# Another constant, in the scheduler's model, for the part of a matmul step that does not depend on its columns

## The chip, the cores and the metric

The kernel runs on one core of one Trainium2 chip. The metric is the device time of one execution in microseconds (us); lower is better. Several runs of the same program are taken and their median is compared. Names of engines: PE is TensorE (PEld its weight loads), DVE VectorE, ACT ScalarE, POOL GpSimd, SP SyncE, which here only issues DMAs.

## The reference

Two layers of a hybrid trunk on 512 tokens of width 2048, in fp32. Each layer normalises x, projects it with one wide matrix, feeds two head groups (a gated linear attention and a chunked softmax attention), concatenates the gated heads, projects them out, normalises again and adds the result to x:

```python
def hybrid_layer(x, w_in, w_out, g_pre, g_post, ...):
    h = rmsnorm(x, g_pre)
    z = h @ w_in
    gq, gk, gv, gg, ga, aq, ak, av, ag = split_columns(z)
    log_a = jax.nn.log_sigmoid(ga @ w_alpha + b_alpha) / GLA_TAU
    o_gla = gla_chunk_causal(gq, gk, gv, log_a)
    o_gla = rmsnorm(o_gla, g_gla) * jax.nn.silu(gg)
    o_att = chunk_band_attention(aq, ak, av, rel_bias)
    o_att = rmsnorm(o_att, g_att) * jax.nn.silu(ag)
    y = jnp.concatenate([o_gla, o_att], axis=-1) @ w_out
    return x + rmsnorm(y, g_post)
```

## The kernel before

**Jobs.** The weights of both layers are cut into blocks, and every piece of 256 x 512 weights is one `Job` (class at line 135). A job has three parts. `load` (L144) issues DMAs on SP: one weight piece into a tile `raw` or `H` (L141) and, for some products, a stored left operand into a tile `sa` (L166). `high` (L168) forms sums of weight pieces on DVE where a product needs them (L176, L178, L180) and casts the result on ACT to a short format, the tile `wh` (L183). `low` (L185) subtracts on DVE what the cast has kept, which gives the tile `wl` (L187). Each product is then three matmuls: left-high by `wh`, left-high by `wl`, left-low by `wh`.

**Products.** `std_gemm` (L266; matmuls at L283) multiplies block by block. `fast_gemm` (L297; matmuls at L347 and L357) takes two column blocks together and forms seven products P1 to P7 of four pieces each in place of eight, with sums of operands formed beforehand. Those sums of left operands lie in DRAM (`S1` to `S4`, `A22`, and `oS...` for the output projection) and come back as the `sa` tiles.

**Other work beside the stream.** Attention heads, the linear attention, the norms and the transposes are Python generators that the gemms advance between jobs. At the end of a layer `finish` (L1118) runs `finish_token` (L1099): a sum of squares (L1101), a reciprocal root on POOL (L403), and four pieces of x + y*r on DVE (L1113). In layer 0 `prep_half` (L448) then normalises the new x (L456), transposes it on PE into one of four PSUM tiles `ax` (L466), evacuates each with two ACT instructions (L476) and splits it (L105, L106) into the left operands `a110`, `a120` and so on of layer 1.

**Two loads that share the SP queue.** `fetch_operands`, called after every piece of the last products of the input projection, loads what the attention heads have written to DRAM (`oa_d`, written at L804 from POOL's queue, one transfer for each two heads) for the output projection:

```python
def fetch_operands(k, c):
    passed.add((k, c))
    for i in range(4):
        if ("P1", 3) in passed and 2 * i in heads_done and (0, i) not in op_att:
            op_att[0, i] = slot(f"a11{i}", [2, 512], F32R)
            nc.sync.dma_start(flat(op_att[0, i]), oa_d[l][0, i])      # L1044
```

Its tiles are named a110 to a113; a112 belongs to heads 4 and 5, whose transfer to DRAM comes last.

**What sets the order.** The program is written once, in the order of the Python text. The framework then orders each engine's own instruction stream:

```python
with tile.TileContext(nc, schedule_with_timeline_sim=True) as tc:   # L1209
    hybrid_trunk(tc, *args)
```

It follows a modelled timeline of all engines and puts next on each engine what the model says comes up next. On the chip every engine works through its stream strictly in that order and waits on semaphores where an input is not there yet. Tile names carry running numbers (`wl_3096`, `sa_1142`), which stay the same when the order changes.

Of the kernel before, what the change touches and what calls it, by code (L numbers as in the profile page):

```python
# [6 lines left out]

F32 = mybir.dt.float32
F32R = mybir.dt.float32r
BF16 = mybir.dt.bfloat16  # L10
# [23 lines left out]
def hybrid_trunk(  # L34
# [29 lines left out]
    def nm(s):  # L64
        serial[0] += 1
        return f"{s}_{serial[0]}"

    def slot(tag, shape, dtype=F32):
        return slots.tile([P] + shape, dtype, tag=tag, name=nm(tag))

    def rtile(tag, shape=(2, W), dtype=F32, bufs=4):
        return ring.tile([P] + list(shape), dtype, tag=tag, name=nm(tag), bufs=bufs)

    def t2(shape=(512,), dtype=F32):
        return tmp.tile([P] + list(shape), dtype, tag="t2", name=nm("t2"))

    def ev():
        return tmp.tile([P, 512], F32, tag="ev", name=nm("ev"), bufs=6)

    def sgt(shape):  # L80
        return tmp.tile([P] + shape, F32, tag="sg", name=nm("sg"), bufs=2)

    def sm(cols, tag="sm", bufs=None):
        return small.tile([P, cols], F32, tag=tag, name=nm(tag), **({"bufs": bufs} if bufs else {}))

# [1127 lines left out]
```

## Time and profile before

| | |
|---|---|
| time, median of 3 runs | 1702.46 us (1696.93, 1702.46, 1706.23) |
| profiled execution, from its first to its last instruction | 1701.1 us; its own time is given only by this span |
| PE busy | 1648.9 us, 97% of the span |
| DVE, ACT, POOL busy | 1209.9, 873.2, 160.0 us |
| mean granted TensorE clock | 0.991 |

How to read the profile's lines: in a timeline a row is start, duration (us), engine, line of the kernel, operation, output<-inputs, count, and in brackets how long the engine sat idle before it and what ended that. A matmul's recorded 0.39 us overlaps its neighbours; the step from one to the next is what counts. The chain of waits is followed back from the last instruction; its rows are start, length and what filled it. The windows view gives, for a stretch of time, its length, each engine's busy time with the number of its instructions, then the granted PE clock, the DMA engines' busy share and GB/s.

### The profile page before, as it was taken

The page shows a single profiled execution, that of the slowest core. Times are in us where ns is not written, and L with a number is a line of the kernel's source. Part 1 is how long each engine was busy: PE and PEld are TensorE (multiplying, and loading weights), DVE is VectorE, ACT ScalarE, POOL GpSimd, SP SyncE. Part 2 cuts the span into 40 slices and gives each one's busy share as a digit, 9 for nine tenths or more (in the row PEclk, how much of TensorE's full clock was granted, in tenths as well). Part 3 has the DMA queues.
Part 4 walks back from the last instruction along what each step waited for, and adds up shares of the span by engine and source line. Part 5 has one row for each costly group of instructions (what it writes and reads, how often), then busy time and mean ns, then how long its engine had stood idle before and what let it go on. Part 6 is the DMA issues. An engine that isn't in the chain of part 4 may idle for free. (4 is left out here: it accounts for less than half of the span.)

```text
span 1701.1 us, 24915 instructions
## 1 busy us (share of the span) xinstructions
PE 1648.9 (97%) x9090; PEld 1403.5 (83%) x9090; DVE 1209.9 (71%) x1563; ACT 873.2 (51%) x1460; POOL 160.0 (9%) x256
## 2 busy tenths in 40 slices
PE   7999999999999999999999999999999999999995
PEld 5888878999987877787778878799999888777884
DVE  5846867686776876468887567668777667854886
ACT  8634544455665544345684345345556555433443
POOL 0210000001000101210122000000001001022101
PEclk8999999999999999999999999999999999999998
DMA  7986877868858797589779688868587678865993
GB/s 259 364 301 226 331 255 265 281 203 273 294 184 279 242 348 252 175 315 314 251 239 370 240 294 297 290 233 291 192 298 256 210 259 268 300 232 197 354 334 135
DMA packets 143002, 455.04 MB, mean 268 GB/s; under 512 B 15444, under 2 KB 32212, under 8 KB 142880
## 3 DMA queue, kind: packets, MB, share of 16 engines
q1 hardware_dynamic: 119984, 373.76, 64.2%
q0 software_dynamic: 22176, 78.41, 11.9%
q8 instruction: 72, 1.18, 0.3%
q10 hardware_dynamic: 720, 1.28, 0.2%
q14 instruction: 50, 0.41, 0.1%
HBM read 381.28 MB, written 72.11 MB: 267 GB/s over the span
## 5 line engine op out<-in xcount | busy, mean ns | idle before, releaser
L357 PE MATMUL mm<-wh,sa 128*128 128x512 f32 x1536 | 490.3, 394 | 9.1 <-ACT wh L183 4.0
L183 ACT CAST wh<-raw 128x1024 fp32r<-128x1024 f32 x248 | 261.8, 1057 | 276.8 <-PE mm L357 76.4
L187 DVE TENSOR_TENSOR wl<-raw,wh 128x1024 fp32r<-128x1024 f32 x248 | 301.8, 1221 | 96.5 <-PE mm L283 32.2
L357 PEld LDWEIGHTS mm<-wh,sa 128*128 128x128 f32 x1536 | 289.7, 189 | 74.5 <-ACT wh L183 5.8
L183 ACT CAST wh<-H 128x1024 fp32r<-128x1024 f32 x224 | 234.8, 1052 | 225.2 <-PE mm L357 123.9
L187 DVE TENSOR_TENSOR wl<-H,wh 128x1024 fp32r<-128x1024 f32 x224 | 272.3, 1221 | 93.8 <-PE mm L357 33.5
L357 PE MATMUL mm<-wl,sa 128*128 128x512 f32 x768 | 303.2, 395 | 9.5 <-DVE wl L187 9.4
L347 PE MATMUL mm<-sa,wh 128*128 128x256 f32 x1280 | 236.9, 285 | 0.0
L347 PEld LDWEIGHTS mm<-sa,wh 128*128 128x128 f32 x1280 | 200.2, 191 | 0.4
L357 PE MATMUL mm<-wh,a 128*128 128x512 f32 x576 | 184.0, 393 | 2.6 <-DVE t L319 2.6
L347 PE MATMUL mm<-sa,wl 128*128 128x256 f32 x640 | 181.3, 283 | 0.0
L357 PEld LDWEIGHTS mm<-wl,sa 128*128 128x128 f32 x768 | 145.4, 189 | 43.5 <-DVE wl L187 14.5
L283 PE MATMUL mm<-wh,a 128*128 128x512 f32 x512 | 169.4, 395 | 3.6 <-ACT a L105 1.8
L176 DVE TENSOR_TENSOR H<-H,raw 128x1024 f32<-128x1024 f32 x112 | 136.7, 1222 | 1.9
L357 PEld LDWEIGHTS mm<-wh,a 128*128 128x128 f32 x576 | 107.3, 188 | 25.1 <-DVE t L319 3.0
L347 PEld LDWEIGHTS mm<-sa,wl 128*128 128x128 f32 x640 | 122.5, 191 | 0.0
L180 DVE TENSOR_TENSOR raw<-H,raw 128x1024 f32<-128x1024 f32 x48 | 58.8, 1225 | 86.1 <-DMA raw<-in_w_dram 86.0
L403 POOL TENSOR_TENSOR sm<-sm,mhalf 128x2 f32<-128x2 f32 (+2 forms) x44 | 53.2, 1210 | 688.6 <-DVE sm L777 459.9
L283 PEld LDWEIGHTS mm<-wh,a 128*128 128x128 f32 x512 | 95.9, 188 | 26.0 <-ACT a L105 2.3
L357 PE MATMUL mm<-wl,a 128*128 128x512 f32 x288 | 113.5, 394 | 0.9 <-DVE wl L187 0.9
L283 PE MATMUL mm<-wl,a 128*128 128x512 f32 x256 | 100.5, 393 | 0.5 <-DVE wl L187 0.4
L347 PE MATMUL mm<-a,wh 128*128 128x256 f32 x512 | 94.8, 284 | 0.0
(193 smaller groups left out, 2350.9 us busy)
## 6 DMA issues: line engine op xcount, KB each, us to landing
raw<-in_w_dram SPq DMA_DIRECT2D x312, 512.0 KB, 5.2
sa<-S SPq DMA_DIRECT2D x192, 512.0 KB, 5.1
H<-in_w_dram SPq DMA_DIRECT2D x56, 512.0 KB, 4.8
sa<-A SPq DMA_DIRECT2D x48, 512.0 KB, 6.0
S<-g POOLq DMA_DIRECT2D x32, 512.0 KB, 7.8
oS<-g POOLq DMA_DIRECT2D x32, 512.0 KB, 7.1
sa<-oS SPq DMA_DIRECT2D x32, 512.0 KB, 5.5
sg<-t POOLq DMA_DIRECT2D x32, 256.0 KB, 5.5
```

The costliest lines, as they stand in the source:

```text
L176: nc.vector.tensor_tensor(out=h, in0=h, in1=r, op=ALU.add)
L180: nc.vector.tensor_tensor(out=r, in0=h, in1=r, op=ALU.subtract)
L183: last_cast[0] = nc.scalar.copy(self.wh, src).ins
L187: nc.vector.tensor_tensor(out=self.wl, in0=self.src, in1=self.wh.bitcast(F32), op=ALU.subtract)
L283: nc.tensor.matmul(pss[o], a[:, part, t], rhs[:, kk, :], start=(i == 0 and kk == 0 and m == 0), stop=(i == n - 1 and kk == 1 and m == 2),)
L347: nc.tensor.matmul(dst, lhs[:, kk, f], a[:, part, tok], start=(fresh and kk == 0 and m == 0 and ft % 2 == 0), stop=(c == 3 and kk == 1 and ...
L357: nc.tensor.matmul(out_ps[t], a[:, part, tok], rhs[:, kk, :], start=(fresh and kk == 0 and m == 0), stop=(c == 3 and kk == 1 and m == 2), ...
L403: nc.gpsimd.tensor_tensor(out=out_r, in0=v, in1=mhalf[:, : v.shape[-1]], op=ALU.pow)
```

## The change

Two lines behind the imports; no line of the kernel's own code changes:

```diff
 from concourse import mybir
 from concourse._compat import with_exitstack
 
+import concourse.hw_specs as _hs
+_hs.TRN2Spec.PE_FULL_CLOCK_PASS_GAP_NS = 13.3
 F32 = mybir.dt.float32
 F32R = mybir.dt.float32r
 BF16 = mybir.dt.bfloat16
```

The constant belongs to the model by which the framework orders the instructions: at PE's full clock a matmul's modelled step is its columns by the clock's period plus this constant. It was 2.5. The same instructions run on the same engines; only their order within an engine's stream moves. Lines of the changed kernel are two higher than before (L357 is L359). With that allowed for, 777 rows of PE's 7,200 odd stand differently, 439 lines of DVE's listing, 212 of ACT's, 64 of SP's and 6 of POOL's. Nearly all are swaps of neighbours. The three places that matter for what follows:

**SP, last products of layer 0's input projection.** Before, the load of a112 stands behind the left operands sa_1142 and sa_1145:

```order
L141 DMA raw_1155_6074<-in_w_dram 128x1024
L166 DMA sa_1142_5998<-S203_91 128x1024
L166 DMA sa_1145_6017<-S402_98 128x1024
L1044 DMA a112_1129_5934<-oa002_158 128x1024
L166 DMA sa_1148_6035<-S403_99 128x1024
```

Now it stands ahead of both:

```order
L143 DMA raw_1155_6074<-in_w_dram 128x1024
L1046 DMA a112_1129_5934<-oa002_158 128x1024
L168 DMA sa_1142_5998<-S203_91 128x1024
L168 DMA sa_1145_6017<-S402_98 128x1024
L168 DMA sa_1148_6035<-S403_99 128x1024
```

Layer 1 has the same move, of a112_2688 ahead of sa_2701 and sa_2704. So SP now reaches sa_1142 and sa_2701 only after the load of a112 has been issued.

**DVE, the last products of layer 1 with the final norms of tokens 0 to 255.** Before (wl_3091, wl_3096 and wl_3104 are the low parts of three consecutive pieces, L178 forms the sum of two pieces that is split next, L1113 the output):

```order
L187 TENSOR_TENSOR wl_3091_15717<-raw_3083_15676,wh_3087_15697 128x1024
L178 TENSOR_TENSOR raw_3088_15699<-raw_3088_15699,raw_3089_15701 128x1024
L1101 TENSOR_REDUCE sm_3102_15755<-ssy_2910_14855 128x1
L1088 TENSOR_TENSOR g1_3077_15652<-t2_3100_15750,t2_3004_15307 128x512
L1101 TENSOR_REDUCE sm_3106_15779<-ssy_2913_14867 128x1
L1113 SCALAR_TENSOR_TENSOR g6_2928_14915<-g8_2911_14857,sm_3103_15756,g6_2928_14915 128x1024
L1113 SCALAR_TENSOR_TENSOR g7_2929_14916<-g0_3074_15646,sm_3103_15756,g7_2929_14916 128x1024
L187 TENSOR_TENSOR wl_3096_15740<-raw_3088_15699,wh_3092_15720 128x1024
L1113 SCALAR_TENSOR_TENSOR g12_2930_14919<-g11_2914_14869,sm_3107_15780,g12_2930_14919 128x1024
L1113 SCALAR_TENSOR_TENSOR g13_2931_14920<-g1_3077_15652,sm_3107_15780,g13_2931_14920 128x1024
L178 TENSOR_TENSOR raw_3093_15722<-raw_3093_15722,raw_3094_15724 128x1024
L187 TENSOR_TENSOR wl_3104_15775<-raw_3093_15722,wh_3097_15743 128x1024
```

Now:

```order
L189 TENSOR_TENSOR wl_3096_15740<-raw_3088_15699,wh_3092_15720 128x1024
L180 TENSOR_TENSOR raw_3093_15722<-raw_3093_15722,raw_3094_15724 128x1024
L1103 TENSOR_REDUCE sm_3102_15755<-ssy_2910_14855 128x1
L1090 TENSOR_TENSOR g1_3077_15652<-t2_3100_15750,t2_3004_15307 128x512
L1103 TENSOR_REDUCE sm_3106_15779<-ssy_2913_14867 128x1
L1115 SCALAR_TENSOR_TENSOR g6_2928_14915<-g8_2911_14857,sm_3103_15756,g6_2928_14915 128x1024
L1115 SCALAR_TENSOR_TENSOR g7_2929_14916<-g0_3074_15646,sm_3103_15756,g7_2929_14916 128x1024
L189 TENSOR_TENSOR wl_3104_15775<-raw_3093_15722,wh_3097_15743 128x1024
L1115 SCALAR_TENSOR_TENSOR g12_2930_14919<-g11_2914_14869,sm_3107_15780,g12_2930_14919 128x1024
L1115 SCALAR_TENSOR_TENSOR g13_2931_14920<-g1_3077_15652,sm_3107_15780,g13_2931_14920 128x1024
L189 TENSOR_TENSOR wl_3108_15799<-H_2975_15128,wh_3105_15777 128x1024
```

The split wl_3096 and the sum raw_3093 have passed the norm's rows, and wl_3104 stands ahead of g12 and g13. Some rows earlier, the sum raw_3070 and one product with the gain (g1_3077) have moved ahead of the split wl_3081. The end of layer 0 has the same moves among its rows.

**PE, from layer 0 to layer 1.** Before, layer 1's first matmuls (wh_1586 by a110) come while eight of the 32 transposes of the first half of the tokens are left, and the other 24 stand in small groups among the matmuls ahead:

```order
L357 MATMUL mm_1450_7468<-wl_1585_8093,g17_1288_6692 128x512
L357 MATMUL mm_1450_7468<-wh_1567_8029,g17_1288_6692 128x512
L283 MATMUL mm_1614_8218<-wh_1586_8095,a110_1563_8002 128x512
L283 MATMUL mm_1614_8218<-wl_1595_8142,a110_1563_8002 128x512
L466 MATMUL ax_1590_8109<-cst_199,g6_1369_7069 128x128
L466 MATMUL ax_1590_8109<-cst_199,g12_1371_7073 128x128
```

Now 31 of the 32 stand in one block between the last matmul of layer 0 and the first of layer 1; its last rows are:

```order
L468 MATMUL ax_1590_8109<-cst_199,g12_1371_7073 128x128
L468 MATMUL ax_1593_8120<-cst_199,g7_1370_7070 128x128
L468 MATMUL ax_1593_8120<-cst_199,g13_1372_7074 128x128
L468 MATMUL ax_1593_8120<-cst_199,g7_1370_7070 128x128
L468 MATMUL ax_1593_8120<-cst_199,g13_1372_7074 128x128
L285 MATMUL mm_1614_8218<-wh_1586_8095,a110_1563_8002 128x512
L285 MATMUL mm_1614_8218<-wl_1595_8142,a110_1563_8002 128x512
```

So wh_1586 now stands behind the whole block, which fills eight PSUM tiles out of a pool of four.

## Prediction

> **What bounds the kernel now.** First the busy shares, then the chain of waits, which says what released whom.
>
> ```profile
> span 1701.1 us, 24915 instructions
> PE 1648.9 (97%) x9090; PEld 1403.5 (83%) x9090; DVE 1209.9 (71%) x1563; ACT 873.2 (51%) x1460; POOL 160.0 (9%) x256
> ...
> 1439.92 7.95 DMA sa<-S
> ...
> 1605.09 19.04 PE mm L357 x84
> ```
>
> PE has 97% of the span, and DVE, the next, 71%. The last row, from the chain, is an undisturbed stretch: 19.04 / 84 = 226.7 ns a matmul of 512 columns. The chain's row above it shows what else can set the end: PE out of work, here for an operand `sa` from DRAM. PE's matmuls are the same before and after, so their time stays; the change can act only through the waits of PE, and the sum below is one of waits. The span is 1701.1 us and the median of the runs 1702.46; the profiled execution is thus an ordinary one, 0.1% under the median, and I sum from 1701.1.
>
> First the constant itself. In the timeline, matmuls of 256 columns follow one another so:
>
> ```profile
> 353.98 0.40 PE L347 MATMUL mm<-sa,wh 128*128 128x256 f32 x2
> 354.22 0.28 PE L347 MATMUL mm<-sa,wl 128*128 128x256 f32 x1
> 354.34 0.40 PE L347 MATMUL mm<-sa,wh 128*128 128x256 f32 x2
> ```
>
> Three steps take 354.34 − 353.98 = 0.36 us, 120 ns each. So 256 more columns cost 226.7 − 120 = 106.7 ns, 512 cost 213.4, and 226.7 − 213.4 = 13.3 ns do not depend on the columns: the changed constant is what this trace says. The Trainium skill (TensorE: Matmul & The Clock Gate, "Wait — 56ns, not 53.3ns?") gives 2.5 ns for this part at full clock and 215.7 ns for 512 columns; the trace's 226.7 does not agree and decides. By the page the old model was right and the new one makes PE look 5% too slow, so that its inputs would be put too late; that is the last rival below. Either way no instruction becomes faster: the number enters the time only through the order.
>
> **A truer model is not yet a better order.** So I went through the moved rows by what each engine does in the trace.
>
> *Most swaps are in slack.* In the middle of the layers sums of weight pieces and small attention products pass a split `wl`. One of the tightest:
>
> ```profile
> 602.24 1.22 DVE L187 TENSOR_TENSOR wl<-raw,wh 128x1024 fp32r<-128x1024 f32 x1
> 603.37 0.42 DVE L106 TENSOR_TENSOR g<-t,g 128x256 fp32r<-128x256 f32 x1
> ...
> 603.72 0.40 PE L357 MATMUL mm<-wl,sa 128*128 128x512 f32 x1
> ```
>
> The split ends at 603.46, its first matmul starts at 603.72: slack 0.26. The product behind it (0.42, about 0.33 in step) now stands ahead, so PE loses under 0.1 us. Five more of these moves have slack close to their delay; elsewhere the delay of 0.6 to 1.2 us meets more slack than that. I put all of the middle at **+0.3**, between −1 (waits of this kind that happen to close) and +2 (six places at 0.33 each).
>
> *SP: a112 ahead of sa_1142 and sa_2701.* Here something real is put in line. The load of a112 reads what POOL's queue writes to `oa`:
>
> ```profile
> L804 POOL DMA_DIRECT2D oa<-g x1: 537/537/537, 602.6 to 602.6; - x1
> ...
> DMA to landing us min/median/max: 3.3/3.3/3.3
> ...
> 603.94 1.09 SPq L166 DMA_DIRECT2D sa<-S  x2
> 605.92 0.32 SPq L1044 DMA_DIRECT2D a<-oa  x1
> 606.34 0.53 SPq L166 DMA_DIRECT2D sa<-S  x1
> ...
> 609.88 0.47 PE L357 MATMUL mm<-wh,sa 128*128 128x512 f32 x1 [1.00 <-DMA sa<-S]
> ```
>
> POOL's transfer starts at 602.6 and lands 3.3 us later, at 605.9; a112 goes out at 605.92. It waits for that landing, and SP stands still meanwhile. Before, sa_1142 had left at 603.94, in front. Now it leaves where today the DMA behind a112 does, at 606.34, 2.4 us later. The last row is its first matmul: PE already sits idle 1.00 us for exactly this load. No slack is left, so if the load takes its 609.88 − 603.94 = 5.94 us again, PE loses 2.4 us. The same in layer 1:
>
> ```profile
> L804 POOL DMA_DIRECT2D oa<-g x1: 537/537/537, 1438.6 to 1438.6; - x1
> ...
> DMA to landing us min/median/max: 3.7/3.7/3.7
> ...
> 1439.92 1.21 SPq L166 DMA_DIRECT2D sa<-S  x2
> 1442.31 0.32 SPq L1044 DMA_DIRECT2D a<-oa  x1
> 1442.76 0.87 SPq L166 DMA_DIRECT2D sa<-S  x1
> ...
> 1448.01 0.51 PE L357 MATMUL mm<-wh,sa 128*128 128x512 f32 x1 [2.56 <-DMA sa<-S]
> ...
> sa<-S SPq DMA_DIRECT2D x192, 512.0 KB, 5.1
> ```
>
> sa_2701 would leave at 1442.76 instead of 1439.92, 2.84 later. It took 8.1 us to its matmul here, because four more transfers shared the DMA engines; the median `sa` takes 5.1 (last row). With 5.1 it would land at 1447.9 and cost nothing; with 8.1 at 1450.9, +2.8. The engines stay as full, so I take **+1.9** here, and **+2.4** for layer 0 (where 5.1 gives +1.6 and 8.1 gives +4.6). The other moves on SP, found by following each load to its first use, have 20 us and more to spare.
>
> *The granted clock.* Behind a long idle PE runs a while at about half clock:
>
> ```profile
> 609.00:613.50 4.50, 3.62 (x16) 2.99 (x17) 3.59 (x4) 2.08 (x3) 0.00 (x0) 1.00 1.03 418
> 1448.00:1451.40 3.40, 3.39 (x9) 2.67 (x10) 2.03 (x2) 0.00 (x0) 0.00 (x0) 0.54 1.02 348
> ```
>
> After 2.56 us of idle the clock was 0.54 for 3.4 us, which costs 3.4 x 0.46 = 1.6 us; after 1.00 us it stayed at 1.00. With 2.4 added, layer 0's idle is 3.4 us, so I add **+1.6** there, from 0 to 1.6. Layer 1 has paid already, and the ends of both layers are such places as well:
>
> ```profile
> 826.00:862.00 36.00, 32.25 (x148) 25.65 (x147) 32.08 (x45) 30.91 (x60) 7.66 (x14) 0.95 0.58 195
> ...
> 1646.00:1690.00 44.00, 37.86 (x157) 29.92 (x155) 33.32 (x39) 16.20 (x27) 3.60 (x7) 0.96 0.50 179
> ```
>
> There 36 x 0.05 and 44 x 0.04, both 1.8 us, go to the clock. The same page of the Trainium skill ("What's actually happening") has the clock fall after an idle window of about 3.4 us; here 2.56 was enough. By the page alone this +1.6 would be open, and the sum 1.6 lower.
>
> *The step from layer 0 to layer 1.*
>
> ```profile
> 830.69 0.80 PE L357 MATMUL mm<-wl,sa 128*128 128x512 f32 x1 [2.56 <-DVE wl L187]
> ...
> 841.50 1.55 ACT L476 ACTIVATE H<-ax,gcol 128x256 f32<-128x256 f32 x4
> ...
> 853.02 0.39 PE L283 MATMUL mm<-wh,a 128*128 128x512 f32 x1
> ...
> 853.48 1.03 PE L466 MATMUL ax<-cst,g 128*128 128x128 f32 x8
> ```
>
> The first idle, 2.56 us at 830.69, is a split that waits behind rows of the norm. With the splits ahead of the norm it shrinks, but the norm ends later and the transposes with it. Eight transposes take 0.8 us in step (853.48 to the next matmul at 854.27), and the other 24 hide among matmuls. Now 31 stand in a row with four PSUM tiles, so the second four need the first evacuated, two ACT instructions each at 1.55 / 4 = 0.39. One round of two tiles is 0.8 of evacuation and 0.8 of transposes; the block costs about 0.1 x 31 = 3.1 us plus some waiting, of which 0.8 was paid already: +2.5, first matmul of layer 1 at about 855.5 instead of 853.02. The low part of a110, a DVE row of 0.69, stands behind norm rows of the next tokens and costs about 1 more; what the earlier idle gives back is about 0.5. I take **+3**, from 0 (all of it regained from the 2.56) to +6.
>
> *The tail.*
>
> ```profile
> 1657.51 1.23 DVE L178 TENSOR_TENSOR raw<-raw,raw 128x1024 f32<-128x1024 f32 x1 [0.31 <-DMA raw<-in_w_dram]
> ...
> 1661.09 1.22 DVE L187 TENSOR_TENSOR wl<-raw,wh 128x1024 fp32r<-128x1024 f32 x1
> ...
> 1664.58 2.48 DVE L1113 SCALAR_TENSOR_TENSOR g<-g,sm,g 128x1024 f32<-128x1024 f32 x2 [0.40 <-POOL sm L403]
> 1666.97 1.22 DVE L187 TENSOR_TENSOR wl<-raw,wh 128x1024 fp32r<-128x1024 f32 x1
> ...
> 1672.89 1.23 DVE L187 TENSOR_TENSOR wl<-raw,wh 128x1024 fp32r<-128x1024 f32 x1 [1.17 <-ACT wh L183]
> ...
> 1668.25 0.49 PE L357 MATMUL mm<-wl,sa 128*128 128x512 f32 x1 [2.57 <-DVE wl L187]
> ...
> 1672.91 0.73 PE L357 MATMUL mm<-wh,sa 128*128 128x512 f32 x2 [2.12 <-ACT wh L183]
> ```
>
> wl_3096 starts at 1666.97 behind two norm rows (2.48) and PE waits 2.57 for it. Putting it ahead would save that. But the move of wl_3081 behind two other DVE rows (1.14 + 0.60 in step) and a later start of the first bring it 2.1 us later; its end frees the buffer of raw_3084, for which the first row above waits already. So the sum raw_3083 comes at about 1659.5, and splits and sums follow: wl_3091 at 1661.9 (+0.8), wl_3096 ends at 1667.2 instead of 1668.2 (−1.0), and wl_3104, now behind g6 and g7 but not g12 and g13, ends at 1674.8 instead of 1674.1. PE's next wait, at 1672.91, goes, and the one for wl_3104 comes in its place. I take **−0.5**, from −3 (the load of raw_3084 is on time all the same) to +1.5.
>
> **Sum:** +0.3 + 2.4 + 1.9 + 1.6 + 3 − 0.5 = +8.7 us; 1701.1 + 8.7 = **1710 us**, 0.5% up. Lower and upper ends of the six terms add to −2.4 and +18.5; I do not expect all on one side.
>
> **Rivals.**
> - *The splits that pass the norms win* (faster). If raw_3084 lands on time and the transposes find their tiles free, the idles of 2.56 at 830.69, 2.57 at 1668.25 and 2.12 at 1672.91 go, and with them the 1.8 of clock at each end: −10.9. With the two a112 terms at their low end (+1.6 and 0) this is −9.3, about **1692**. For it: these are the largest waits on DVE. Against: in both places the norm has to be done before what is next, and its rows are only moved.
> - *The queue on SP is not felt* (no change). If the `oa` transfer lands earlier, or the loads take 5.1 us, what stays is 1.6 + 0.3 and small change at the ends of the layers: about **1703**. Against: idle of 1.00 and 2.56 at just these loads.
> - *The block of transposes stalls PE long enough to lose the clock* (slower still). It decides from about 2.5 us of idle at one place: the boundary at +6 in place of +3, and 1.8 of clock there and in the tail: 8.7 + 3 + 3.6, about **1716**. Against: today's eight transposes in a row cost no idle.
> - *PE's inputs come too late everywhere*, if the shorter step were the true one. The waits of PE for splits now:
>
> ```profile
> PE mm L357 <- DVE wl L187: 10.4, 13, 2.6
> ...
> PE mm L357 <- ACT wh L183: 4.2, 4, 2.1
> ```
>
> That is 14.6 us at 17 places; doubled, **1716**. The measured step of 226.7 ns speaks against it. This is what would follow from the Trainium skill's 2.5 ns (the same page and section).
>
> **How the numbers follow.** Forecast (+4 to +14 us) 0.50; no change 0.23; faster 0.14; lost clock 0.08; too late 0.05. A measurement of this kernel can tell about 0.5%, 8.5 us, from no change. Of the forecast's case a little over half lies above that, so slower has 0.29 + 0.08 + 0.05 = 0.42; faster has 0.10 of its 0.14; within 0.5% is the rest, 0.48. For 8 in 10 the range takes in the forecast, no change, a part of the faster case and the lost clock: 1696 to 1721.
>
> **What will show it.** In the changed profile: SP's a112 issued near 606 with sa_1142 behind it, and the idle at its first matmul near 3.4 us, with a half-clock stretch (right), or still near 1.0 (wrong); the same near 1448 with 4 to 5 us; first L285 matmul of layer 1 near 855.5 plus the earlier shift; idle at wl_3096 near 1.5. Wrong would be: the long idles of both layer ends gone, or the loads of `oa` landing before SP comes to a112.

## The result: 1% slower

Timed against the kernel before, the changed kernel has a ratio of **1.0107**, 95% interval 1.0076 to 1.0138: a median of 1720.13 us (four runs, 1713.74 to 1721.7) beside 1702.16 (four runs, 1696.93 to 1706.23). That is 18 us slower where +8.7 was forecast; the time lies inside the range of the prediction, near its upper end. The profiled execution has a span of 1718.1 us, 17.0 more than before.

The page of the changed kernel:

```profile
span 1718.1 us, 24924 instructions
PE 1653.4 (96%) x9090; PEld 1406.2 (82%) x9090; DVE 1211.8 (71%) x1563; ACT 873.7 (51%) x1460; POOL 154.7 (9%) x256
```

Each engine works through as many instructions as before, and DVE and ACT are as busy (1209.9 and 873.2 before). PE is busy 4.5 us longer (1648.9 before), at a mean granted clock of 0.988 where it was 0.991; the other 12.5 of the 17 us are idle time of PE. Which waits grew is seen first off PE, in the view of waits (engine, line, what was waited for: us in total, times, longest). Before:

```profile
DVE raw L180 <- DMA raw<-in_w_dram: 86.0, 43, 5.1
DVE H L190 <- DMA raw<-in_w_dram: 29.2, 28, 2.1
ACT bias L709 <- DMA bias<-in_rel_dram: 18.2, 12, 2.2
...
PE mm L357 <- DMA sa<-S: 3.8, 3, 2.6
```

and after (lines are two higher):

```profile
DVE raw L182 <- DMA raw<-in_w_dram: 84.3, 41, 5.9
DVE H L192 <- DMA raw<-in_w_dram: 46.4, 32, 4.6
ACT bias L711 <- DMA bias<-in_rel_dram: 23.3, 12, 4.8
...
PE mm L359 <- DMA sa<-S: 7.7, 2, 4.2
```

DVE's sums H (L192) now wait 17 us longer for their loads, and ACT's rows of `bias` 5 us longer; the longest single waits have doubled, from 2.1 and 2.2 to 4.6 and 4.8. On an engine that works in order, whatever stands behind such a row waits too. The last row is PE at the loads behind a112, 7.7 us after 3.8.

To place the difference, PE's time between rows that stand at the same position in both orders was subtracted, stretch by stretch (us of before's span; after minus before). Such a difference holds both the waits and a lower clock:

| place | after − before | the prediction's term |
|---|---|---|
| 600–618 and 1439–1457, SP's a112 | +4.4, +2.1 | +4.0 (with the clock), +1.9 |
| 818–928, layer 0 to layer 1 | +5.3 −0.4 −0.6 = +4.3 | +3 |
| from 1640, tail | −0.3 | −0.5 |
| six places in the middle: 325–345 (+2.8), 426–446 (+1.8), 697–717 (+1.3), and their twins in layer 1, 1154–1194 (+1.9), 1254–1274 (+1.4), 1546–1567 (+1.3) | +10.4 | |
| all the rest of the middle | −3.9 | middle in all: +0.3 |

What the prediction had worked out one by one came out near its terms. The middle, put down as one lump of slack, did not.

**a112.** SP's rows of the changed kernel (start, us), then PE's first matmuls of sa_1142 and sa_2701 with the idle before them, then the clock behind them (length, busy times, granted clock, DMA share, GB/s):

```profile
608.72 0.32 SPq L1046 DMA_DIRECT2D a<-oa  x1
609.13 1.53 SPq L168 DMA_DIRECT2D sa<-S  x3
...
1456.02 0.32 SPq L1046 DMA_DIRECT2D a<-oa  x1
1456.43 1.52 SPq L168 DMA_DIRECT2D sa<-S  x3
```

```profile
616.09 0.76 PE L359 MATMUL mm<-wh,sa 128*128 128x512 f32 x1 [4.19 <-DMA sa<-S]
...
1463.44 0.76 PE L359 MATMUL mm<-wh,sa 128*128 128x512 f32 x1 [3.50 <-DMA sa<-S]
```

```profile
614.00:620.00 6.00, 3.91 (x11) 3.13 (x12) 4.01 (x4) 0.04 (x1) 0.00 (x0) 0.72 0.79 297
1462.00:1467.00 5.00, 3.56 (x9) 2.81 (x10) 2.02 (x2) 0.00 (x0) 0.00 (x0) 0.55 1.00 388
```

The load of a112 leaves first, the three of `sa` 0.41 us behind it, and the idles are 4.19 and 3.50 where they were 1.00 and 2.56. Layer 0 now has its stretch of low clock too: 6.00 x 0.28 = 1.7 us, where 1.6 had been put down. (That such a stretch follows an idle of this length is not certain; see the last section.)

**The layer boundary and the tail**, PE's rows with an idle before them, and the first matmul of layer 1 (864.61):

```profile
828.04 0.73 PE L359 MATMUL mm<-wh,sa 128*128 128x512 f32 x2 [1.72 <-ACT wh L185]
...
838.65 0.50 PE L359 MATMUL mm<-wl,sa 128*128 128x512 f32 x1 [1.17 <-DVE wl L189]
...
844.66 0.80 PE L359 MATMUL mm<-wl,sa 128*128 128x512 f32 x1 [1.94 <-DVE wl L189]
861.91 2.85 PE L468 MATMUL ax<-cst,g 128*128 128x128 f32 x16 [0.89 <-ACT H L478]
864.61 0.50 PE L285 MATMUL mm<-wh,a 128*128 128x512 f32 x1
...
866.33 0.73 PE L285 MATMUL mm<-wh,a 128*128 128x512 f32 x2 [0.52 <-DVE a L108]
...
1685.42 0.50 PE L359 MATMUL mm<-wl,sa 128*128 128x512 f32 x1 [1.18 <-DVE wl L189]
1691.31 0.80 PE L359 MATMUL mm<-wl,sa 128*128 128x512 f32 x1 [1.93 <-DVE wl L189]
```

The transposes (L468) wait 0.89 us for ACT's evacuation, the first matmul of layer 1 comes behind their block, and the fifth (866.33) waits 0.52 for the low part of a110. The idle at wl_1537 (838.65), 2.56 before, is 1.17; those of 1.72 at 828.04 and 1.94 at the next piece, wl_1545 (844.66; 0.52 before), have come in. In the tail the idles of 2.57 and 2.12 became 1.18, at wl_3096, and 1.93, at wl_3104.

**The middle.** Three swaps, each of two layers. At 337, DVE: the sum H_419, which needs a piece of the weights from DRAM, now stands ahead of the split wl_508. Further up, the sum H_409 (325.71) has passed a row of the gemm (L321), and a product with the gate (330.92) has passed the split wl_502 (331.52).

```profile
325.71 1.23 DVE L192 TENSOR_TENSOR H<-H,raw 128x1024 f32<-128x1024 f32 x1 [2.47 <-DMA raw<-in_w_dram]
...
330.92 0.68 DVE L108 TENSOR_TENSOR g<-t,g 128x512 fp32r<-128x512 f32 x1
331.52 1.22 DVE L189 TENSOR_TENSOR wl<-raw,wh 128x1024 fp32r<-128x1024 f32 x1
...
336.87 1.23 DVE L192 TENSOR_TENSOR H<-H,raw 128x1024 f32<-128x1024 f32 x1 [1.74 <-DMA raw<-in_w_dram]
338.01 1.22 DVE L189 TENSOR_TENSOR wl<-raw,wh 128x1024 fp32r<-128x1024 f32 x1
```

DVE stands still for 1.74 us with the split wl_508 ready behind the sum. PE waited 0.92 for wl_502 (at 332.79) and 0.48 for wl_508 (at 339.29). Before, wl_508 ran first, and the wait of the sum, 1.10, left no wait on PE:

```profile
325.94 1.23 DVE L190 TENSOR_TENSOR H<-H,raw 128x1024 f32<-128x1024 f32 x1 [1.56 <-DMA raw<-in_w_dram]
...
333.60 2.35 DVE L187 TENSOR_TENSOR wl<-raw,wh 128x1024 fp32r<-128x1024 f32 x2
337.06 1.23 DVE L190 TENSOR_TENSOR H<-H,raw 128x1024 f32<-128x1024 f32 x1 [1.10 <-DMA raw<-in_w_dram]
```

At 428, ACT: the row of the attention's `bias`, which waits for a load, now stands ahead of a cast, a gate row and the copy t2_741 (L755). Behind it is PE's row that waits:

```profile
427.84 0.63 ACT L711 ACTIVATE bias<-bias 128x512 f32<-128x512 f32 x1 [4.81 <-DMA bias<-in_rel_dram]
428.38 1.03 ACT L185 CAST wh<-raw 128x1024 fp32r<-128x1024 f32 x1
429.32 0.62 ACT L111 ACTIVATE g<-t 128x512 fp32r<-128x512 f32 x1
429.85 0.56 ACT L755 COPY t<-ax 128x512 f32<-128x512 f32 x1
...
430.46 1.16 PE L769 MATMUL ax<-g,t 128*128 128x128 f32 x8 [1.34 <-ACT t L755]
```

ACT waits 4.81 us for the load, and 1.34 of it reaches PE. Before, the copy came first and `bias` after it:

```profile
424.14 0.57 ACT L753 COPY t<-ax 128x512 f32<-128x512 f32 x1
426.19 0.63 ACT L709 ACTIVATE bias<-bias 128x512 f32<-128x512 f32 x1 [1.48 <-DMA bias<-in_rel_dram]
```

At 721, DVE: the split wl_1345 waits for a buffer that PE frees, now ahead of the two gate rows (L975) that PE's small products need:

```profile
720.61 1.23 DVE L189 TENSOR_TENSOR wl<-raw,wh 128x1024 fp32r<-128x1024 f32 x1 [1.68 <-PE mm L285]
721.75 0.87 DVE L975 SCALAR_TENSOR_TENSOR sg<-ax,sm,sg 128x256 f32<-128x256 f32 x2
...
722.33 0.89 PE L985 MATMUL ax<-cst,sg 128*128 128x128 f32 x4 [1.09 <-issue]
```

The view names no releaser for the last row; it starts just behind the end of the first of the two gate rows, near 721.75 + 0.87 / 2 = 722.2. Before, the gate rows came first, and neither the split nor PE's products waited:

```profile
713.62 1.23 DVE L187 TENSOR_TENSOR wl<-raw,wh 128x1024 fp32r<-128x1024 f32 x1
...
714.58 0.60 PE L983 MATMUL ax<-cst,sg 128*128 128x128 f32 x4
```

### The profile page after: what moved, and what is told of

The parts are those of the page before. It is cut to its first block, busy times and chain, and to the rows that moved or that the text cites. A ratio compares the mean times of both kernels' runs of the same rounds, so it can differ in the third digit from the quotient of the medians.

```text
span 1718.1 us, 24924 instructions
## 1 busy us (share of the span) xinstructions
PE 1653.4 (96%) x9090; PEld 1406.2 (82%) x9090; DVE 1211.8 (71%) x1563; ACT 873.7 (51%) x1460; POOL 154.7 (9%) x256
## 3 DMA queue, kind: packets, MB, share of 16 engines
q8 instruction: 72, 1.18, 0.3%
## 4 chain that ended last, share of the span: by engine, by line
PE 80%; DMA 8%; DVE 6%; issue 3%; ACT 2%; POOL 0%; SPq 0%; DVEq 0%; ACTq 0%; POOLq 0%
PE mm L359 36%; PE mm L285 20%; PE mm L349 15%; DMA raw<-in_w_dram 7%; DVE wl L189 3%; PE ax L769 2%; PE ax L923 1%; PE ax L957 1%; PE ax L607 1%; PE ax L752 1%; DMA sa<-S 1%; ACT wh L185 1%; DVE t L321 1%; PE ax L732 1%; PE ax L733 1%
## 5 line engine op out<-in xcount | busy, mean ns | idle before, releaser
L359 PE MATMUL mm<-wh,sa 128*128 128x512 f32 x1536 | 492.6, 396 | 9.9 <-DMA sa<-S 7.7
L359 PEld LDWEIGHTS mm<-wh,sa 128*128 128x128 f32 x1536 | 291.3, 190 | 74.9 <-issue 10.0
L359 PE MATMUL mm<-wl,sa 128*128 128x512 f32 x768 | 303.9, 396 | 10.0 <-DVE wl L189 9.9
L359 PE MATMUL mm<-wh,a 128*128 128x512 f32 x576 | 184.3, 393 | 1.9 <-DVE t L321 1.9
L359 PEld LDWEIGHTS mm<-wl,sa 128*128 128x128 f32 x768 | 146.4, 191 | 43.8 <-DVE wl L189 14.5
L178 DVE TENSOR_TENSOR H<-H,raw 128x1024 f32<-128x1024 f32 x112 | 136.6, 1221 | 1.9
L359 PEld LDWEIGHTS mm<-wh,a 128*128 128x128 f32 x576 | 108.0, 188 | 24.8 <-DVE t L321 2.2
L359 PE MATMUL mm<-wl,a 128*128 128x512 f32 x288 | 113.0, 392 | 3.1 <-DVE wl L189 3.1
L405 POOL TENSOR_TENSOR sm<-sm,mhalf 128x2 f32<-128x2 f32 (+2 forms) x44 | 47.6, 1082 | 723.7 <-DVE sm L779 463.2
L192 DVE TENSOR_TENSOR H<-H,raw 128x1024 f32<-128x1024 f32 x56 | 68.5, 1223 | 46.6 <-DMA raw<-in_w_dram 46.4
```

The costliest lines, as they stand in the source:

```text
L178: nc.vector.tensor_tensor(out=h, in0=h, in1=r, op=ALU.add)
L192: nc.vector.tensor_tensor(out=h, in0=h, in1=self.src, op=ALU.add)
L359: nc.tensor.matmul(out_ps[t], a[:, part, tok], rhs[:, kk, :], start=(fresh and kk == 0 and m == 0), stop=(c == 3 and kk == 1 and m == 2), ...
L405: nc.gpsimd.tensor_tensor(out=out_r, in0=v, in1=mhalf[:, : v.shape[-1]], op=ALU.pow)
```

## Experiments

**Theory one:** the 18 us are PE's waits at these places, tied to the swaps there, and they add up. Each swap put a row whose own input comes late (a load, a buffer) ahead of a row that PE needs. **Rivals:** the middle costs nothing, and what is seen there is the variation of one profile; or a constant of 13.3 ns makes any order worse.

To take the order of one part alone, eight kernels (and `gains`, below) fix the order of every engine's instructions by edges that set only the order of issue and add no wait. `_ORDER` holds for each engine the numbers of its instructions, from before's stream with some stretches of after's, or the reverse:

```diff
         hybrid_trunk(tc, *args)
+        _rows = {int(i.name[2:]): i for i in nc.cur_bb.bb.instructions if i.name.startswith("I-")}
+        for _seq in _ORDER:
+            _seq = [n for n in _seq if n in _rows]
+            for _a, _b in zip(_seq, _seq[1:]):
+                tc.add_manual_dep(_rows[_b], _rows[_a].name,
+                    mybir.DependencyInfo(mybir.DependencyClass.NoSync, mybir.DependencyReason.DATA), reason="order")
```

Below, the diff of each is that of `_ORDER`. The first four were timed against a median before of 1699.76 us. Differences in us are the measured ratio times that median; the difference of the two medians can be another (8.4 us for mid_only, where the ratio gives 11.9).

**sp_only**: before, with a112 ahead in both layers and nothing else.

```diff
+DMA a112_1129_5934<-oa002_158 128x1024
 DMA sa_1142_5998<-S203_91 128x1024
 DMA sa_1145_6017<-S402_98 128x1024
-DMA a112_1129_5934<-oa002_158 128x1024
```

> The kernel of before with every engine's order held as it was, except SP: the load of a112 stands ahead of the two sa loads in both layers (six rows). Theory one (a row that is moved forward brings the wait for its own input with it, and what stands behind it in the same queue waits along): the idle of PE at sa_1142 grows from 1.0 to about 4.2 us with a stretch at half clock, that at sa_2701 from 2.6 to about 3.8, as in the changed kernel; together +4 and +1.5, so 1707.5 us, 5 to 6 us over before. Rival (the idle of PE there comes from the new order as a whole, with the attention and the DMA load of its surroundings): within 2 us of before.

Measured: 1704.97 us, ratio 1.0029 (1.0012 to 1.0046), that is +4.9 us (2.0 to 7.8). The rows of layer 0:

```profile
604.78 0.32 SPq L1046 DMA_DIRECT2D a<-oa  x1
605.19 1.45 SPq L168 DMA_DIRECT2D sa<-S  x3
```

```profile
611.26 0.47 PE L359 MATMUL mm<-wh,sa 128*128 128x512 f32 x1 [2.43 <-DMA sa<-S]
```

The swap costs time by itself. The idle grew by 1.43 and not 2.4: `sa` left 605.19 − 603.94 = 1.25 us later, since a112 itself could leave at 604.78.

**sp_back**: after, with those rows back (the same diff, reversed).

> The changed kernel with every engine's order held as it is, except SP: a112 goes back behind the two sa loads in both layers. Theory one: the same 5 to 6 us come off, 1714 to 1715 us, with about 1.0 and 2.6 us of idle left at sa_1142 and sa_2701. Rival: the idle stays and the time with it, 1720.

Measured: 1710.95, ratio to before 1.0079 (1.0049 to 1.0109). Against after's 1.0107 this is 0.0028, 4.8 us less. Each of the two ratios is known to 0.003 only, so this alone is not clear of zero; it agrees with sp_only, on which the 5 us rest.

**bound_only**: before, with after's order from 800 to 905 us on all engines; of PE's rows, for one:

```diff
+MATMUL ax_1590_8109<-cst_199,g12_1371_7073 128x128
+MATMUL ax_1593_8120<-cst_199,g7_1370_7070 128x128
 MATMUL mm_1614_8218<-wh_1586_8095,a110_1563_8002 128x512
 MATMUL mm_1614_8218<-wl_1595_8142,a110_1563_8002 128x512
-MATMUL ax_1590_8109<-cst_199,g12_1371_7073 128x128
```

> The kernel of before, and only from 800 to 905 us of its profile, the step from layer 0 to layer 1, the order of the changed kernel on all engines. By the prediction's term +3 us (0 to 6); by the comparison of the two profiles +4: about 1706 us. Rival (the block of transposes and the split are paid by what the earlier idle gives back): within 1 us of before.

Measured: 1701.21, ratio 1.0016 (0.9993 to 1.0040): +2.7 us, from −1.2 to +6.8. It agrees with the predicted +3, and does not exclude zero. The profiles help: reckoned by place as above, 818–928 shows +1.9 to +4.3 in the four kernels with after's order there (after, sp_back, bound_only, three_back) and −1.7 to +1.8 in six with before's order, means +3.1 and 0.0.

**mid_only**: before, with all of after's order but for a112, 800 to 905 us and the tail from 1640 us.

> The kernel of before with the order of the changed kernel on all engines in the rest: everything ahead of 800 us and from 905 to 1640 us, without the two moves of a112. By the prediction's term +0.3 us (-1 to +2), about 1702.5. By theory one, read from the two profiles, this is where the prediction falls short: +7 to +8, about 1709.5, in single idles of 0.5 to 2 us where PE waits for attention steps and splits that stand behind rows waiting for a DMA.

Measured: 1708.13, ratio 1.0070 (1.0045 to 1.0095): +11.9 us (7.7 to 16.1). The prediction's +0.3 for the middle is refuted; the +7 to +8 read from the two profiles was low as well. The three parts add to 4.9 + 2.7 + 11.9 = 19.5 us, and after is 18 slower: they add up as far as their intervals, of some 3 to 4 us each way, can tell.

The next four split the middle (before: 1700.76 us). **three_only**: before, with after's order only at the six places (322–346, 419–452, 704–718 us, and 1158–1192, 1255–1289, 1543–1559 in layer 1). The decisive rows, two on DVE and one on ACT:

```diff
 TENSOR_TENSOR wl_505_2991<-raw_495_2923,wh_503_2963 128x1024
+TENSOR_TENSOR H_419_2362<-H_419_2362,raw_510_3027 128x1024
 TENSOR_TENSOR wl_508_3022<-raw_504_2965,wh_506_2994 128x1024
-TENSOR_TENSOR H_419_2362<-H_419_2362,raw_510_3027 128x1024
...
+TENSOR_TENSOR wl_1345_6983<-raw_1322_6862,wh_1337_6939 128x1024
 SCALAR_TENSOR_TENSOR sg_1327_6904<-ax_1339_6957,sm_1341_6963,sg_1327_6904 128x256 x2
-TENSOR_TENSOR wl_1345_6983<-raw_1322_6862,wh_1337_6939 128x1024
...
+ACTIVATE bias_723_4119<-bias_723_4119 128x512
 CAST wh_730_4186<-raw_726_4152 128x1024
 ACTIVATE g12_732_4190<-t2_736_4194 128x2x256
 COPY t2_741_4215<-ax_740_4210 128x512
-ACTIVATE bias_723_4119<-bias_723_4119 128x512
```

> The kernel of before with the changed kernel's order, on PE, DVE, ACT and SP, at three places of each layer only: 322 to 346, 419 to 452 and 704 to 718 us of its profile and the same in layer 1 (1158 to 1192, 1255 to 1289, 1543 to 1559). Theory one (what is lost in the middle is lost where rows with a late input of their own were moved ahead): these six places hold nearly all of it, +2.1, +2.1 and +1.5 in layer 0 and about the same in layer 1 from the profiles so far, +11 us, 1711. Rival (the loss of the middle is spread over all moved rows, each a little too late): a share of it like the share of the rows, 235 of 1271 on PE, +2 us, 1702.

Measured: 1711.07, ratio 1.0063 (1.0041 to 1.0085): +10.7 us (7.0 to 14.5).

**three_back**: after, with the six places as before.

> The changed kernel with the order of before at those six places. Theory one: -11 us from the changed kernel, 1707 to 1709 us. Rival: -2 us, 1718.

Measured: 1705.04, ratio to before 1.0019 (1.0000 to 1.0037). Of after's 18 us, 15 are gone. By these two runs the six places carry some 11 to 15 of the 18 us. The kept profiles say the same by place: against before, the six places together cost +10.4 us in after and +9.7, +12.6 and +13.2 in the other kernels with after's order there (mid_only, sp_back, three_only), and 0.0 in each of three with before's order there (sp_only, bound_only, gains). So it is not the variation of one profile.

**three_dveact**: the six places on DVE, ACT and SP only.

> The kernel of before with the changed kernel's order at those six places on DVE, ACT and SP alone; PE's order is that of before. Theory one, in the form that the queues of DVE and ACT are what blocks (the sum H_419 ahead of wl_508, the load-fed bias row ahead of the copy t2_741, the split wl_1345 ahead of the gate sg_1327): the same +11 us, or a little less. Rival (PE's own attention steps have been put ahead of their inputs): within 2 us of before.

Measured: 1709.19, ratio 1.0054 (1.0036 to 1.0073): +9.2 us.

**three_pe**: the six places on PE only.

> The kernel of before with the changed kernel's order at those six places on PE alone. Theory one in that form: within 2 us of before. Rival (PE's own attention steps have been put ahead of their inputs): most of the +11 us.

Measured: 1704.72, ratio 1.0022 (1.0004 to 1.0039): +3.7 us. That is more than theory one had in this form (within 2 us), and far less than its rival (most of 11). By time the queues of DVE and ACT carry the larger part. PE's own order costs something too when the others don't follow: an attention product is reached before its gate rows are there.

```profile
340.27 0.50 PE L731 MATMUL ax<-g,g 128*128 128x512 f32 x1 [1.34 <-ACT g L107]
341.96 0.50 PE L732 MATMUL ax<-g,g 128*128 128x512 f32 x1 [1.18 <-DVE g L108]
```

So the 9.2 and the 3.7 are not shares of one sum; each is what one side costs with the other unmoved. By place the two differ: PE's order alone costs 3.6 + 4.1 us at H_419 and its twin, more than DVE's and ACT's alone (1.9 + 1.1), and nothing at bias_723 and its twin, where theirs costs 1.7 + 1.3. In three_pe the six places show +9.4 and the span only +1.1; where the rest came back was not followed up.

**Why would a truer model put rows with late inputs ahead?** A guess: the model also thinks that loads land sooner than they do. With PE's step too short, everything that PE needs was called for too early, and that covered the error. The last four kernels test this, timed against a median of 1699.78 us. The first two let the scheduler make its own order.

**slow_dma**: the 13.3 ns, and a modelled delay from a DMA's issue to its start that is 1.5 us longer on every queue.

```diff
 _hs.TRN2Spec.PE_FULL_CLOCK_PASS_GAP_NS = 13.3
+_hs.TRN2Spec.DGE_DMA_DELAY = {e: t + 1500 for e, t in _hs.TRN2Spec.DGE_DMA_DELAY.items()}
```

> The change's 13.3 ns stays, and one more figure of the scheduler's model is altered: the delay from a DMA's issue to its start is 1.5 us longer on every queue. The order that comes out has the loads of a112 behind sa_1142 and sa_2701 again, the sum H_419 behind wl_508 again, and bias_723 behind the copy t2_741 again; wl_1345 stays ahead of the gate rows sg_1327. Theory one (rows with late inputs were put ahead because the model, with a truer matmul step alone, thought their loads had landed): the change's cost of +18 us loses about 4.6 us at H_419 and its twin of layer 1, 3.2 at bias_723 and its twin, 4.8 at a112; +2.6 at wl_1345 and its twin stays, and so does part of the boundary: about +5 against the kernel before, that is 1704 to 1709. Rival (it is the constant as such: any order that the scheduler makes with 13.3 ns is worse, since some 1,670 rows of TensorE still stand elsewhere): 1714 or more.

Measured: **1689.23 us, ratio 0.9939 (0.9916 to 0.9962)**: 10 us faster than before, and 29 less than with the 13.3 ns alone (0.9939 against 1.0107). The waits:

```profile
DVE raw L183 <- DMA raw<-in_w_dram: 34.8, 31, 3.3
DVE H L193 <- DMA raw<-in_w_dram: 19.6, 22, 2.6
```

DVE's two sums wait 54 us for their loads where they waited 115 before (86.0 + 29.2) and 131 after. The rival is refuted: it is not the constant as such. By place, the costs at H_419, bias_723, a112 and their twins are gone (within 0.1 of zero at 319–355, 409–428, 1166–1184 and 1256–1274, −0.6 at 600–618), and wl_1345, which this delay does not move back, still costs what it did, +1.3 in each layer. The forecast of 1704 to 1709 was too high all the same: it counted what the longer delay takes back, and not what it improves in the kernel before. The loads of `sa` and a112 (595.21 and 598.54) and the copy and `bias` (419.43 and 421.29) stand in before's order again.

**slow_dma_only**: the longer delay without the change.

```diff
-_hs.TRN2Spec.PE_FULL_CLOCK_PASS_GAP_NS = 13.3
+_hs.TRN2Spec.DGE_DMA_DELAY = {e: t + 1500 for e, t in _hs.TRN2Spec.DGE_DMA_DELAY.items()}
```

> The kernel before's constant, and the 1.5 us longer delay from a DMA's issue to its start in the scheduler's model alone. The order keeps a112, H_419, bias_723 and wl_1345 where the kernel before has them; some 980 rows of TensorE stand elsewhere. Theory one: nothing with a late input is put ahead, so within 4 us of the kernel before (1698 to 1706). Rival (any rearranging of the tuned order costs some 10 us, because the order of before is by chance a good one): 1710 or more.

Measured: 1692.86, ratio 0.9970 (0.9956 to 0.9984), 5 us faster than before; below the range expected, and the rival is refuted. The waits:

```profile
DVE H L192 <- DMA raw<-in_w_dram: 13.8, 14, 2.1
...
DVE raw L182 <- DMA raw<-in_w_dram: 8.6, 13, 1.9
```

Here DVE waits 22 us for loads. PE's stops for splits at 154 and 233 us, 1.00 and 0.70 us of idle before, do not appear in either of these two kernels; they stand in the profiles of all the others. The first is of the same kind, in the kernel before already: the splits stand behind a sum that waits for its load.

```profile
151.94 1.23 DVE L180 TENSOR_TENSOR raw<-H,raw 128x1024 f32<-128x1024 f32 x1 [4.47 <-DMA raw<-in_w_dram]
153.08 2.35 DVE L187 TENSOR_TENSOR wl<-H,wh 128x1024 fp32r<-128x1024 f32 x2
```

Beside the longer delay the 13.3 ns costs nothing: 1689.23 with it and 1692.86 without. That it gains there is not settled, since the two intervals overlap.

**const_7p5**: the constant at 7.5 ns.

```diff
-_hs.TRN2Spec.PE_FULL_CLOCK_PASS_GAP_NS = 13.3
+_hs.TRN2Spec.PE_FULL_CLOCK_PASS_GAP_NS = 7.5
```

> The constant at 7.5 ns in place of 13.3. In the order that comes out H_419 is ahead of wl_508 and bias_723 ahead of the copy t2_741 (though behind the gate rows g12_732), as after the change; a112 and wl_1345 stand as before. Theory one: about +2 to +4.6 at H_419 and its twin, +1 to +3.2 at bias_723 and its twin, nothing at a112 and wl_1345, and perhaps +2 at the boundary: 1704 to 1710. Rival (the cost grows with the distance of the constant from 2.5 ns, in proportion: 5.0 of 10.8 ns, so 46% of +18): 1708 to 1711; the two differ by place more than by sum: by the rival a share of every place's cost is there, wl_1345's too.

Measured: 1700.58, ratio 1.0015 (0.9995 to 1.0035): less than either expected. By place H_419 and its twin cost 1.0 + 1.9 us, as theory one said; wl_1345, which is not moved here, costs nothing, against the rival. But bias_723, ahead of its copy here too, costs only 0.4 with its twin: it stands behind the gate row now, and its load has all but landed:

```profile
423.99 0.63 ACT L111 ACTIVATE g<-t 128x512 fp32r<-128x512 f32 x1
425.13 0.63 ACT L711 ACTIVATE bias<-bias 128x512 f32<-128x512 f32 x1 [0.52 <-DMA bias<-in_rel_dram]
425.67 0.57 ACT L755 COPY t<-ax 128x512 f32<-128x512 f32 x1
```

This fits a cost that lies less in the swap of two rows than in how long the forward one still waits: 0.52 us here, 4.81 with 13.3 ns. (With 13.3 ns a cast and the gate row stand behind it as well, so the two orders differ by more than this wait.)

**gains**: before, with after's order only where after's profile gained: 500–602 (without a112), 740–800, 1340–1438 and from 1579 us on. One such piece is wl_3096 ahead of the final norm, in the tail.

```diff
+TENSOR_TENSOR wl_3096_15740<-raw_3088_15699,wh_3092_15720 128x1024
+TENSOR_TENSOR raw_3093_15722<-raw_3093_15722,raw_3094_15724 128x1024
 TENSOR_REDUCE sm_3102_15755<-ssy_2910_14855 128x1
...
-TENSOR_TENSOR wl_3096_15740<-raw_3088_15699,wh_3092_15720 128x1024
```

> The kernel before, with the changed kernel's order taken only in those stretches of the program in which the changed kernel's profile gained: 500 to 602 us (but for a112), 740 to 800, 1340 to 1438, and from 1579 to the end, on TensorE, VectorE, ScalarE and SyncE. Theory one (the change's cost and gains are tied to places, and add up): -0.6 at 566 to 586, -1.5 to -2.4 at 778 to 798, -1.0 at 1376 to 1439, -0.3 at 1607, -0.3 in the tail: 3 to 5 us faster than the kernel before, a ratio of 0.997 to 0.998. Rival (the gains were the variation of single profiles, or are taken back at the next DMA wait): within 1.5 us.

Measured: 1695.61, ratio 0.9977 (0.9960 to 0.9994): 3.9 us faster than before, as expected. The change has good moves, and they can be had without the bad ones. Its profile shows the gains at 566–586, 1376–1439 and 1579–1640 again (−0.6, −1.1 and −0.3); the −2.4 at 778–798 is in part variation, since two kernels with before's order there show −1.6 and −1.8. The lowest median of all kernels here is slow_dma's, which beats both the kernel before and the changed one.

## Why the prediction was right and wrong

- **The bound** (PE; the change acts only through PE's waits): right in the main. DVE, ACT and the count of instructions stayed as they were, and every experiment moved the time by order alone. Of the 17 us of the profile 4.5 are PE's busy time, by the lower clock.
- **The constant** (13.3 ns is what the trace says): it holds for the 256 and 512 columns from which it was worked out. It does not cover the 128 columns of the transposes, whose step is about 0.1 us (0.79 us for eight at 853.48 before), where 106.7 / 2 + 13.3 = 67 ns would follow; whether their type or their weight loads make the difference was not looked into. "A truer model is not yet a better order" held; with the longer delay of the loads the same 13.3 ns costs nothing beside that delay alone.
- **"Most swaps are in slack", +0.3 for the middle: wrong, and the step that failed.** Alone the middle costs 11.9 us (7.7 to 16.1), six places of it 10.7. The step held the delay of a moved row, 0.6 to 1.2 us, against the slack of the row behind it. That counts the duration of the row that moves ahead, and not the wait for its own input that it brings along: 1.74 us at H_419, 4.81 at bias_723, 1.68 at wl_1345. For a112 the same question was asked (what does it wait for, and who stands behind?), and there the answer held; it was not asked on DVE and ACT, where the page of before already had 29.2 and 18.2 us of such waits, on just these lines. One stop is half of the kind that was counted: wl_502 comes 0.97 us later (331.52 in place of 330.55), behind one more product with the gate (0.6 in step), but also behind the row of the gemm that now stands behind the sum H_409 and its wait for a load (2.47 us); PE was idle 0.92.
- **a112, +2.4, +1.9, and +1.6 for the clock:** right in mechanism and about right in size. Forecast 5.9, measured 4.9 alone (2.0 to 7.8). The row left later, as said, and the idles of 4.19 and 3.50 stand beside the forecast 3.4 and "4 to 5". That these two numbers came so near is in part luck: bound_only, which does not move a112, has idles of 3.43 and 3.18 there, and at 600–618 the seven kernels of fixed order that leave a112 behind the two loads show −0.7 to +3.5 us against before, the three kernels with the move +2.3 to +4.4.
- **The boundary, +3:** the trace gives +4.3, the run 2.7 (−1.2 to +6.8). The first matmul of layer 1 came at 864.61, 11.6 later than before, of which 6.4 were there at 818. The other 5.2 are more than the +2.5 put down for the block of transposes, but not all of them are the block: the idles of 1.72 and 1.94 ahead of it count too. About 1 us was regained by 928, and the low part of a110 cost PE 0.52 where about 1 was put down. That the 2.56 of idle would shrink was right for that piece (1.17) and wrong for the place, since wl_1545 behind it now waits 1.94.
- **The tail, −0.5:** −0.3, with wl_3096 and wl_3104 as described.
- **The sum:** without the middle's term the forecast had +8.4, and the trace has 4.4 + 2.1 + 4.3 − 0.3 = +10.5. With the middle as mid_only measured it, 11.9 in place of 0.3, the forecast would have been +20. That 1720 still lies inside the range is owed to the range's width: its upper part was given to the lost clock, which is not what happened.
- **The rivals.** "The splits that pass the norms win": no, the longest idles at both layer ends are 1.94 and 1.93 now and did not vanish. "SP not felt": no, by sp_only. "Lost clock": the boundary stayed at +4.3; the number was near, not the reason. "PE's inputs come too late everywhere": its sign was that PE's 14.6 us of waits for the splits on L357 would double; there are 15.5 now (13.0 for `wl` and 2.5 for `wh`, after 10.4 and 4.2). What comes late is not everywhere but at places with a row that waits. The Trainium skill's 2.5 ns (TensorE: Matmul & The Clock Gate, "Wait — 56ns, not 53.3ns?"), from which that rival came, does not agree with the trace's steps of 226.7 and 120 ns. The times do not decide between the two figures: const_7p5 is within measurement of before, after is slower, and slow_dma, with 13.3, is faster.

What stays open: whether the model's loads are too early by 1.5 us, or by how much; that a longer delay helps is shown, and its best size was not sought. What slow_dma pays at the layer boundary (+5.0 at 856–874, where PE waits 2.69 us for wl_1621) was not followed up.

## What to carry to other kernels

When a scheduler's order moves a row ahead, ask of that row what it waits for and how long, and only then how long it runs: on an engine that works in order, as these do here, its wait passes to all that stand behind it. The view of waits on the engines that are not the bound already lists such rows. Two errors of a model may cover each other, so that making one figure truer alone costs time. Here changing a second figure as well, the delay of the loads, gave back what the first had cost and more; that the second is truer for it was not shown.

## What the runs showed of the hardware

- The same load, sa_1142 or sa_2701, took from 5.9 to 8.6 us from its issue to its first matmul over 14 profiles, though the transfers are the same: 5.9 to 7.3 with a112's load ahead of it (six values), 5.9 to 8.6 without (22 values). Part of the later issue came back that way. Why was not looked into.
- An idle of PE of 4.19 us brought a stretch at 0.72 of the clock over 6 us (614 to 620), and 3.50 us one at 0.55 over 5 us: 6.00 x 0.28 = 1.7 and 5.00 x 0.45 = 2.3 us, as 2.56 of idle cost 1.6 before. An idle of 1.00 had brought none. But the length of the idle alone does not settle it: in three_back, 3.23 us at 611.48 left the clock at 1.00 from 608 to 620, and in sp_only 1.32 us at 540.08 was followed by 0.50 from 540 to 543.4. The +1.6 of the prediction for layer 0 was thus a likely cost, not a sure one.
